# Transposed blocks in two alternating tiles, transposed one to two steps sooner: a two-layer encoder on one Trainium2 core

## The chip, the cores and the metric

The kernel runs on one core of a Trainium2 chip. A core has a matrix engine (TensorE, PE in the profile), a vector engine (VectorE, DVE), an engine for activations and casts (ScalarE, ACT), GpSimd (POOL) and SyncE (SP). Each works through its own queue in order, and they wait for each other by semaphores. Transfers between the core's memory and the device's run on 16 DMA engines; SP issues most of them and GpSimd those that add to what lies at the target. Beside ScalarE, VectorE and GpSimd prepare operands and TensorE multiplies into banks of its accumulator memory, which the others empty.

The metric is the device time in microseconds (us) of one execution; the median of several runs counts.

## What is computed

A sequence of 512 tokens with 1024 features passes two layers. The first has a stick-breaking attention, the second a gated linear recurrence; both end in the same multilayer perceptron (MLP), and a last norm follows. Cut to what matters here:

```python
for layer in range(DEPTH):
    h = rms_norm(x, norm_mix[layer])
    y = mixer(layer, h)
    x = x + y
    h = rms_norm(x, norm_mlp[layer])
    x = x + squared_relu_mlp(h, mlp_w1[layer], mlp_w2[layer])
return rms_norm(x, norm_final)

def squared_relu_mlp(h, w1, w2):
    u = jax.nn.relu(h @ w1)
    return (u * u) @ w2
```

The change lies in the second layer's MLP, at `x = x + ...`: the `x` that is added there.

## The kernel before

**Numbers.** Everything is float32. A product is made of three matmuls with operands split into a high half (a cast on ScalarE) and a low half (operand less high half, on VectorE), lines 242 to 246 and 1079 to 1086. So every 512 KB of weights cost a cast of 1.05 us on ScalarE and a subtraction of 1.2 us on VectorE.

**The MLP (class `Mlp`).** The 4096 hidden features are taken in four quarters of 1024. Quarter one's hidden features are computed ahead of the loop. Then `run` (line 1156) walks a list of 98 steps: 14 "down" steps of quarter one (steps 0 to 13), and for each further quarter 14 "up" steps (`h @ w1`, hidden features; two parts of seven products) and 14 "down" steps (`@ w2`). Quarter two has steps 14 to 41, quarter three 42 to 69, quarter four 70 to 97. The place of a step is counted here from its quarter's first: step 45 has place 3. The products follow a scheme of Strassen's kind: seven products P1 to P7 of quarter-size blocks stand for eight, with sums of operands before and sums of results after. In the up steps they come as P1, P5, P6, P3, P7, P2, P4, at places 0 to 6 for the first part and 7 to 13 for the second.

**One step.** For step i the loop (line 1344) calls `load(i)`, then `leave(i - 1)`, then issues TensorE's matmuls of step i. `load(i)` first runs what stands in the dictionary `aside` for step i, then issues due weight loads. `leave(i - 1)` empties the result of the step before (copies and relus on ScalarE, sums of results on VectorE, into tile `u`; later low halves go to `bl` and `sl`) and prepares the weight operand of step i + 3, with its cast (`wh`), its low half (`wl`), the sum of two weight blocks for the next product (`b<-b,b` on VectorE) or an addition to a weight block by DMA from GpSimd (line 1101). From the middle of quarter one, VectorE's and ScalarE's instructions of this loop are held in the order in which they are written (class `Ordered`, which gives line 786 to all of them in the profile). SP's and GpSimd's queues are ordered by the scheduler.

**The blocks of x.** The MLP's inputs and hidden features lie with features along partitions; the results `c` (`mlp.y(t, h)`) lie with tokens along partitions. So `x`, which has to be added to the result, must be transposed. It is parked in the device's memory (`away`, line 1667) while the MLP begins, and comes back in eight blocks of 128 tokens by 512 features, each in three stages, all hung into `aside` by the loop at line 1697:

- `fetch(n, a)`, four times: SP brings a quarter of block n back as pieces of 32 by 32, so placed that a transposition inside each 32 by 32 square completes the whole. Even blocks come to the end of `bh`, odd ones to the end of `bl`.
- `turned(n)`: VectorE transposes the 32 by 32 squares into a tile (`blocks`), 128 by 512 numbers. Before, this was one tile for all, of tag `osum` with one buffer.
- `joined(n)`, two steps later: GpSimd issues a DMA of 256 KB that adds the tile to the result (`c<-blocks` in the profile).

`BY_BLOCKS` holds for each block (first step of its fetches, fetches per step, step of its turn). As one tile serves all blocks, the turn of block n + 1 cannot start before the copy (`joined`) of block n has landed; and a fetch to `bh` or `bl` waits for the turn two blocks before. A turn stands in VectorE's order ahead of everything that `leave` of the step before issues.

Of the kernel before, what the change touches and what calls it, by code (L numbers as in the profile page):

```python
# [12 lines left out]
F32 = mybir.dt.float32  # L13
# [5 lines left out]
P = 128  # L19
S = 512  # L20
D = 1024
C = D // P
# [8 lines left out]

BLOCK = 32
BY_BLOCKS = (
    (12, 2, 16), (14, 1, 19), (17, 1, 23), (29, 1, 43), (33, 1, 46), (44, 1, 50), (57, 1, 71), (61, 1, 74),
)
START = [
# [31 lines left out]
def hybrid_encoder(  # L68
# [28 lines left out]
    work = ctx.enter_context(tc.tile_pool(name="work", bufs=2))  # L97
# [212 lines left out]
    HOMES = (*(("keep", 4),) * 4, *(("w3", 3),) * 3, ("osum", 1))  # L310

    def home_tile(tag, n, name):
        return home.tile([P, S], F32, tag=tag, name=name, bufs=n)
# [1349 lines left out]
    with ExitStack() as mctx:  # L1663
# [4 lines left out]
        blocks = {}  # L1668
# [18 lines left out]

        def turned(n):

            to = home_tile(*HOMES[C - 1], "blocks")  # L1690
            mlp.V.transpose(out=to, in_=blocks[n])
            blocks[n] = to

# [3 lines left out]
        for n, (at, by, done) in enumerate(BY_BLOCKS):  # L1697
            for a in range(P // BLOCK):
                mlp.aside.setdefault(at + a // by, []).append(partial(fetch, n, a))
            mlp.aside.setdefault(done, []).append(partial(turned, n))  # L1700
            mlp.aside.setdefault(done + 2, []).append(partial(joined, n))
# [171 lines left out]
```

## Time and profile before

| | us |
|---|---|
| median of 3 runs (1030.94 to 1031.68) | 1031.47 |
| the profiled execution | 1032.85 |
| its span, first to last instruction | 1031.0 |
| TensorE busy | 1019.2 |
| VectorE busy | 858.9 |
| ScalarE busy | 715.2 |
| the eight transpositions, each | 0.70 to 0.71 |
| the eight copies `c<-blocks`, issue to landing | 4.0 to 9.2, median 5.7 |

The copies, in order of blocks, took 8.6, 6.9, 4.0, 9.2, 5.5, 4.7, 5.9 and 4.6 us from issue to landing.

How to read the rows: a row of the timeline has the start and the length in us, the engine, the line of the kernel, the operation, what is written and read with the size, the count, and in brackets how long the engine idled before it and which instruction ended that wait. A row of the chain has start, length, engine, tile and line. "DMA to landing" gives the least, the median and the most us from issue to landing of the transfers that were asked for. In a row of windows there are, behind the stretch and its length, the busy time and count of TensorE's matmuls, its weight loads, VectorE, ScalarE and GpSimd, then the granted clock of TensorE, the DMA engines' busy share and GB/s. On VectorE and ScalarE the next instruction often starts a tenth before the one ahead ends.

### The profile page before, as it was taken

Reading aid. Unit: us, or ns where it says so; the run is one execution under the profiler, and the core shown is the slowest. Engines: PE = TensorE matmul, PEld = TensorE weight load, DVE = VectorE, ACT = ScalarE, POOL = GpSimd, SP = SyncE. Lnnn points to the kernel's source line nnn. Section 1 sums busy time; section 2 is a strip of 40 time slices with the busy share of each in tenths; the row PEclk is TensorE's granted clock in tenths of the full one; section 3 lists DMA queues with packets and bytes.
Section 4 is the critical chain, followed back from the end, with each engine's and each line's share of the span. In section 5 each row is a group of like instructions: output and inputs, shape, how many; then the busy total and the mean of one; then the engine's idle time right before and its main releaser. Section 6 shows DMA issues by size and latency. Waiting matters only on the chain.

```text
span 1031.0 us, 15905 instructions
## 1 busy us (share of the span) xinstructions
PE 1019.2 (99%) x5836; PEld 888.6 (86%) x5836; DVE 858.9 (83%) x1152; ACT 715.2 (69%) x1110; POOL 180.6 (18%) x243
## 2 busy tenths in 40 slices
PE   9999999999999999999999999999999999899997
PEld 7888888888878988988988888888888988888986
DVE  7888787847897798898899889984877898798898
ACT  6777676835877774874875689964876774674865
POOL 0354444420010010010012111300011111111112
PEclk9999999999999999999999999999999999999999
DMA  7845454537546677677682574364457977977753
GB/s 234 219 121 144 110 151 105 152 109 268 150 92 185 165 165 194 169 153 195 166 226 82 147 169 124 103 232 152 107 108 199 213 167 197 189 159 196 185 122 107
DMA packets 71902, 165.72 MB, mean 161 GB/s; under 512 B 23824, under 2 KB 25104, under 8 KB 71824
## 3 DMA queue, kind: packets, MB, share of 16 engines
q1 hardware_dynamic: 59424, 123.54, 37.7%
q0 software_dynamic: 11680, 40.38, 23.2%
q8 instruction: 46, 0.75, 0.3%
q10 hardware_dynamic: 720, 0.79, 0.2%
q14 instruction: 32, 0.26, 0.1%
HBM read 139.51 MB, written 6.29 MB: 141 GB/s over the span
## 4 chain that ended last, share of the span: by engine, by line
PE 87%; DVE 6%; ACT 3%; DMA 3%; issue 2%; SPq 0%; DVEq 0%; ACTq 0%
PE ps_t L1119 15%; PE ps_acc L1119 8%; PE ps_acc L1024 7%; PE ps_z L1024 6%; PE ps_acc L244 5%; PE ps_acc L246 5%; PE ps_acc L245 5%; PE ps_z L1119 4%; PE ps_o L1024 3%; PE ps_t L244 2%; PE ps_t L245 2%; PE ps_t L246 2%; PE ps_o L244 2%; PE ps_o L245 2%; PE ps_o L246 2%
## 5 line engine op out<-in xcount | busy, mean ns | idle before, releaser
L786 DVE TENSOR_TENSOR wl<-b,wh 128x1024 fp32r<-128x1024 f32 x168 | 203.9, 1219 | 48.7 <-ACT wh L786 47.7
L786 ACT CAST wh<-b 128x1024 fp32r<-128x1024 f32 x168 | 174.1, 1050 | 99.4 <-DVE b L786 57.3
L1101 POOL DMA_DIRECT2D b<-in_w_dn x40 | 35.1, 877 | 336.0 <-DVE b L786 143.7
L244 PE MATMUL ps_acc<-xg,wh 128*128 128x512 f32 x200 | 81.7, 408 | 0.0
L1024 PE MATMUL ps_z<-xg,wh 128*128 128x256 f32 x384 | 79.2, 278 | 1.8 <-ACT u L786 1.7
L246 PE MATMUL ps_acc<-xg,wh 128*128 128x512 f32 x200 | 78.4, 392 | 0.0
L245 PE MATMUL ps_acc<-xg,wl 128*128 128x512 f32 x200 | 78.4, 392 | 0.0
L239 DVE TENSOR_TENSOR wl<-raw,wh 128x512 fp32r<-128x512 f32 (+2 forms) x70 | 61.6, 905 | 16.2 <-ACT wh L237 16.1
L786 ACT ACTIVATE u<-u 128x512 f32<-128x512 f32 x100 | 63.2, 632 | 15.2 <-DVE u L786 13.5
L609 DVE TENSOR_TENSOR_SCAN scan<-keep,later 128x128 f32<-128x128 f32 (+1 forms) x64 | 58.7, 919 | 17.1 <-ACT keep L599 10.7
L237 ACT CAST wh<-raw 128x512 fp32r<-128x512 f32 (+2 forms) x70 | 50.7, 759 | 24.6 <-PE ps_acc L246 7.3
L1024 PE MATMUL ps_z<-xg,wl 128*128 128x256 f32 x240 | 66.4, 277 | 0.0
L1024 PEld LDWEIGHTS ps_z<-xg,wh 128*128 128x128 f32 x384 | 62.8, 188 | 2.4 <-ACT u L786 2.4
L1024 PE MATMUL ps_acc<-xg,wh 128*128 128x256 f32 x288 | 61.5, 277 | 1.1 <-ACT u L786 1.1
L613 POOL TENSOR_TENSOR w<-w,scan 128x128 f32<-128x128 f32 (+1 forms) x64 | 51.7, 809 | 53.8 <-DVE scan L609 50.8
L786 DVE TENSOR_TENSOR b<-b,b 128x1024 f32<-128x1024 f32 x48 | 58.7, 1223 | 1.3
L1101 POOL DMA_DIRECT2D b<-in_w_up x24 | 20.9, 871 | 215.6 <-DMA b<-in_w_up 86.3
L786 DVE TENSOR_TENSOR u<-u 128x512 f32<-128x512 f32 (+1 forms) x92 | 54.7, 594 | 2.4 <-ACT u L786 1.1
L1024 PE MATMUL ps_acc<-xg,wl 128*128 128x256 f32 x192 | 53.1, 276 | 0.0
L786 ACT CAST wh<-raw 128x1024 fp32r<-128x1024 f32 x46 | 47.9, 1044 | 7.3 <-PE ps_acc L1119 7.3
L1024 PE MATMUL ps_acc<-low,wh 128*128 128x256 f32 x192 | 53.0, 276 | 0.0
L1119 PE MATMUL ps_t<-wh,sl 128*128 128x512 f32 x126 | 49.3, 392 | 0.3 <-DVE sl L786 0.3
(372 smaller groups left out, 3276.2 us busy)
## 6 DMA issues: line engine op xcount, KB each, us to landing
b<-in_w_dn SPq DMA_DIRECT2D x48, 512.0 KB, 5.0
b<-in_w_dn POOLq DMA_DIRECT2D x40, 512.0 KB, 5.6
b<-in_w_up SPq DMA_DIRECT2D x36, 512.0 KB, 4.4
b<-in_w_up POOLq DMA_DIRECT2D x24, 512.0 KB, 5.5
raw<-in_w_m SPq DMA_DIRECT2D x16, 512.0 KB, 4.5
raw<-in_w_dn SPq DMA_DIRECT2D x16, 512.0 KB, 4.7
raw<-in_w_in SPq DMA_DIRECT2D x16, 512.0 KB, 4.4
raw<-in_w_qk SPq DMA_DIRECT2D x12, 512.0 KB, 3.8
```

Of the source, the lines that this page charges most:

```text
L237: A.copy(wh[:, k, :], raw[:, k, :])
L239: V.tensor_tensor(wl[:, k, :], raw[:, k, :], f(wh[:, k, :]), ALU.subtract)
L244: PE.matmul(ps, wh, ah, start=start, stop=False)
L245: PE.matmul(ps, wl, ah, start=False, stop=False)
L246: PE.matmul(ps, wh, al, start=False, stop=stop)
L609: V.tensor_tensor_scan(sc[:, S - n : S][:, ::-1], keep[:, :n][:, ::-1], later[:, S - n :][:, ::-1], 1.0, ALU.mult, ALU.max,)
L613: G.tensor_tensor(wt, wt, sc[:, S - n + 1 : S + 1], ALU.mult)
L786: ins = getattr(self.e, name)(*args, **kwargs)
L1024: PE.matmul(ps[:, i * HS : (i + 1) * HS], m, y, start=new and i == k == n == 0, stop=i == 1 and k == C // 2 - 1 and n == 2, skip_group_che ...
L1101: G.dma_start(out=unit[b].rearrange("p j n -> p (j n)"), in_=unit["src"](to), accum_op=ALU.add)
L1119: PE.matmul(ps, m, y[:, jj, cols], start=first and n == 0, stop=last and n == 2, skip_group_check=not new,)
```

## The change

Blocks with an odd number are transposed into a tile of another tag, `ssq`, with one buffer, which served the sum of squares before the loop. Even blocks keep the tile of before. Five of the eight turns come one or two steps sooner, and with each its copy, which stays two steps behind.

```diff
 BY_BLOCKS = (
-    (12, 2, 16), (14, 1, 19), (17, 1, 23), (29, 1, 43), (33, 1, 46), (44, 1, 50), (57, 1, 71), (61, 1, 74),
+    (12, 2, 16), (14, 1, 18), (17, 1, 21), (29, 1, 43), (33, 1, 45), (44, 1, 48), (57, 1, 71), (61, 1, 73),
 )
@@
         def turned(n):
 
-            to = home_tile(*HOMES[C - 1], "blocks")
+            if n % 2:
+                to = work.tile([P, S], F32, tag="ssq", name="blocks", bufs=1)
+            else:
+                to = home_tile(*HOMES[C - 1], "blocks")
             mlp.V.transpose(out=to, in_=blocks[n])
             blocks[n] = to
```

In places: block 0 stays at 2, block 1 goes from 5 to 4, block 2 from 9 to 7 (quarter two); block 3 stays at 1, block 4 goes from 4 to 3, block 5 from 8 to 6 (quarter three); block 6 stays at 1, block 7 goes from 4 to 3 (quarter four).

## The prediction

> **What bounds the kernel now.** I read the page first, for the bound of the whole, then the timeline of TensorE in layer two's multilayer perceptron, to measure its quarters one against the other.
>
> ```profile
> PE 1019.2 (99%) x5836; PEld 888.6 (86%) x5836; DVE 858.9 (83%) x1152; ACT 715.2 (69%) x1110; POOL 180.6 (18%) x243
> PE 87%; DVE 6%; ACT 3%; DMA 3%; issue 2%; SPq 0%; DVEq 0%; ACTq 0%
> ...
> 788.91 0.28 PE L1024 MATMUL ps_acc<-xg,wh 128*128 128x256 f32 x1
> ...
> 866.83 0.28 PE L1024 MATMUL ps_acc<-xg,wh 128*128 128x256 f32 x1
> ...
> 947.25 0.28 PE L1024 MATMUL ps_acc<-xg,wh 128*128 128x256 f32 x1
> ...
> 961.06 2.72 PE ps_z L1024 x24
> ```
>
> TensorE is the bound, and the chain leaves it for some 13% of the span. The three matmul rows are the first ones of steps 14, 42 and 70, so quarter two lasts 866.83 - 788.91 = 77.92 us and quarter three 80.42. A step is 24 matmuls in 2.72 us (last row), and 28 steps are 76.16. So quarter two loses 1.76 us and quarter three 4.26. That is the most that these two can give. Where quarter three loses them stands in the timelines of VectorE, TensorE and GpSimd:
>
> ```profile
> 872.05 0.89 POOL L1695 DMA_DIRECT2D c<-blocks  x1 [2.21 <-DVE blocks L786]
> ...
> DMA to landing us min/median/max: 9.2/9.2/9.2
> ...
> 876.81 1.23 DVE L786 TENSOR_TENSOR wl<-b,wh 128x1024 fp32r<-128x1024 f32 x1 [0.36 <-ACT wh L786]
> 881.29 0.71 DVE L786 STREAM_TRANSPOSE blocks<-bh 128x512 f32<-128x512 f32 x1 [3.25 <-DMA c<-blocks]
> 881.92 0.65 DVE L786 TENSOR_TENSOR u<-ps_acc,u 128x512 f32<-128x512 f32 x1
> ...
> 884.43 0.38 PE L1024 MATMUL ps_acc<-xg,wh 128*128 128x256 f32 x1 [1.06 <-ACT u L786]
> ...
> 893.89 0.39 PE L1024 MATMUL ps_z<-xg,wh 128*128 128x256 f32 x1 [0.99 <-ACT u L786]
> ...
> 900.33 0.39 PE L1024 MATMUL ps_z<-xg,wh 128*128 128x256 f32 x1 [0.71 <-ACT u L786]
> ```
>
> The turn of block 4 idles VectorE for 3.25 us: it writes the one tile that the copy of block 3 (issued at 872.05, landed 9.2 later, at 881.25) still reads. Behind it, in VectorE's fixed order, stands the subtraction of step 45, whose product TensorE had ended at 866.83 + 4 x 2.72 = 877.71. ScalarE follows with the relu, and TensorE then waits three times for a bank that ScalarE empties late. The three waits are 2.76 us; the first matmuls behind each, slower than the rest, and tenths elsewhere make up the 4.26.
>
> How much lateness VectorE may have is read by laying quarter four over it, where nothing waits for a copy:
>
> ```profile
> 957.23 1.23 DVE L786 TENSOR_TENSOR wl<-b,wh 128x1024 fp32r<-128x1024 f32 x1 [0.36 <-ACT wh L786]
> 958.48 0.71 DVE L786 STREAM_TRANSPOSE blocks<-bl 128x512 f32<-128x512 f32 x1
> 959.11 0.65 DVE L786 TENSOR_TENSOR u<-ps_acc,u 128x512 f32<-128x512 f32 x1
> ...
> 833.53 0.68 DVE L786 TENSOR_TENSOR sl<-u,sh 128x512 fp32r<-128x512 f32 x1
> ...
> 913.95 0.68 DVE L786 TENSOR_TENSOR sl<-u,sh 128x512 fp32r<-128x512 f32 x1
> ...
> 990.55 0.68 DVE L786 TENSOR_TENSOR sl<-u,sh 128x512 fp32r<-128x512 f32 x1
> 991.33 0.46 PE L1119 MATMUL ps_t<-wh,sl 128*128 128x512 f32 x1
> 991.63 0.40 PE L1119 MATMUL ps_t<-wh,sh 128*128 128x512 f32 x1
> ```
>
> Counted from each quarter's first matmul, the low half `sl` that the third down step needs starts at 44.62, 47.12 and 43.30 us. Quarter four's TensorE meets it almost without a gap (990.55 + 0.68 = 991.23, then 991.33 and 991.63). So VectorE and ScalarE, which hand work to each other from the first subtraction to this one, have no slack over TensorE there: what a turn adds to their chain, TensorE loses. Quarter three is 3.82 us behind quarter four, quarter two 1.32.
>
> **The change part by part.** Nothing is added in number: eight turns and eight copies stay, each turn 0.63 us from its start to the next instruction (881.29 to 881.92). Odd blocks get their own tile, and five turns move.
>
> *Block 4, place 4 to 3.* It now waits for the copy of block 2, over since long, and stands before the instruction at 876.81. VectorE idled there from 876.45, so the turn fills those 0.36 us, and the weight's low half starts at 876.45 + 0.63 = 877.08. From such a low half to the subtraction it is 1.15 us where nothing comes between (800.30 to 801.45, below), so that starts at 878.23, after the 877.71 of TensorE. Against 881.92 that is **3.69 us earlier**.
>
> *Block 5, place 8 to 6.*
>
> ```profile
> 888.49 0.68 DVE L786 TENSOR_TENSOR u<-u,ps_z 128x512 f32<-128x512 f32 x1
> 889.74 1.23 DVE L786 TENSOR_TENSOR wl<-b,wh 128x1024 fp32r<-128x1024 f32 x1 [0.58 <-ACT wh L786]
> ...
> 895.25 0.70 DVE L786 STREAM_TRANSPOSE blocks<-bl 128x512 f32<-128x512 f32 x1
> 895.88 2.83 DVE L786 TENSOR_TENSOR u<-u 128x512 f32<-128x512 f32 x4
> ```
>
> Before, it stood in a stretch without idle time and cost its whole 0.63. Now it stands ahead of 888.49, with 0.58 us of VectorE's idle time right behind. The low half at 889.74 does not move; ScalarE's relu, which needs the sum of 888.49, becomes some 0.2 us later. So it costs 0.2 (between 0 and 0.63). Together the `sl` of quarter three comes at 913.95 - 3.69 - 0.43 = 909.83, that is 43.00 after its first matmul, 0.30 before quarter four's. TensorE then no longer pays the 3.82 by which quarter three was behind quarter four. I take **3.7 us gained**, as some tenth may stay, between 3.1 (the turn is not absorbed) and 4.1 (all but 0.16 of the 4.26).
>
> *Block 7, place 4 to 3.* The same move without a wait: 957.23 - 0.36 + 0.63 + 1.15 puts the subtraction of 959.11 at 958.65, 0.46 earlier. But quarter four has only 991.63 and two like gaps of a tenth behind it to win: **0.2 gained**, between 0 and 0.5.
>
> *Block 1, place 5 to 4.*
>
> ```profile
> 800.30 1.23 DVE L786 TENSOR_TENSOR wl<-b,wh 128x1024 fp32r<-128x1024 f32 x1 [1.77 <-ACT wh L786]
> 801.45 0.68 DVE L786 TENSOR_TENSOR u<-ps_acc,u 128x512 f32<-128x512 f32 x1
> ...
> 803.30 1.23 DVE L786 TENSOR_TENSOR b<-b,b 128x1024 f32<-128x1024 f32 x1
> 804.44 0.70 DVE L786 STREAM_TRANSPOSE blocks<-bl 128x512 f32<-128x512 f32 x1
> ...
> 805.64 1.23 DVE L786 TENSOR_TENSOR wl<-b,wh 128x1024 fp32r<-128x1024 f32 x1
> ...
> 804.55 1.06 ACT L786 CAST wh<-b 128x1024 fp32r<-128x1024 f32 x1 [0.61 <-DVE b L786]
> ```
>
> Here the move looks bad. The turn was free: it ran at 804.44 while VectorE would have waited for ScalarE's cast (804.55 to 805.61) anyway. Now it stands ahead of 801.45, and the addition of 803.30, the cast and the low half of 805.64 all come 0.63 later. No idle time of VectorE follows that takes it up, since the chain runs hand to hand. **0.6 lost**, between 0 and 0.63.
>
> *Block 2, place 9 to 7.* It moves from behind the four sums to ahead of the low half before them. VectorE's total is the same; ScalarE's cast of the sums comes 0.63 later, and the bank it then empties too, so a small wait of TensorE grows there, but the later `sl` decides: 0, between 0 and 0.63 lost.
>
> *Queues.* The copies come one or two steps earlier on GpSimd's queue, and the fetches behind them on SP's. SP's fetch for blocks 3, 4, 6 and 7 waits for turns 1, 2, 4 and 5, so it too is issued up to 4 us earlier. On SP that can only free what stands behind it. The transfers join weights in a dense stretch; I take 0 and price it as a rival.
>
> One page of the Trainium skill disagrees with the row that all hangs on. DMA: Bandwidth & Descriptors, section Anatomy of one DMA, gives 2.0 us plus bytes / 436e3 for a DMA of GpSimd's queue. By an estimate from it, 256 KB land in 2.6 us, block 3's copy would have been over at 874.7, and the second tile would gain nothing. The trace has 9.2 and the 3.25 of waiting, and the measurement decides.
>
> The sum: -3.7 - 0.2 + 0.6 = **-3.3 us**. The profiled execution (1032.85, span 1031.0) would become 1029.55 with a span of 1027.7; it lies 1.38 over the median of 1031.47, from which I forecast 1031.47 - 3.3 = 1028.2.
>
> **The rivals.**
>
> *A new wait of block 5 (10%).* Its turn moves to 888.49 - 3.69 = 884.80.
>
> ```profile
> L1681 SPq DMA_DIRECT2D bl<-away x4: 326/484/691, 871.7 to 873.3; - x4
> ...
> DMA to landing us min/median/max: 6.3/8.3/8.9
> ...
> 885.37 0.87 POOL L1101 DMA_DIRECT2D b<-in_w_up  x1 [2.09 <-DVE b L786]
> ...
> DMA to landing us min/median/max: 5.6/5.6/5.6
> ...
> 895.37 1.05 ACT L786 CAST wh<-b 128x1024 fp32r<-128x1024 f32 x1
> ...
> 800.00:815.00 15.00, 15.00 (x134) 14.98 (x133) 12.56 (x13) 11.98 (x18) 2.64 (x3) 1.00 0.99 222
> ```
>
> Its four fetches are issued from 871.7 to 873.3 (first row) and land after 8.9 at most: by 882.2. The tile it now shares with block 3 is free at 881.25. The slack is 2.6 us. Were the landings 4 us longer, TensorE would lose 1.4 and the time be 1029.6. Against it: what competes is issued later than the fetches.
>
> *Quarter two pays nothing (12%).* If the 0.63 is hidden after all, as in its old place: 1031.47 - 3.9 = 1027.6.
>
> *Slower: the weight additions come late (8%).* In the dense stretches (DMA busy 0.99 from 800 to 815) earlier fetches and copies push back the additions that GpSimd issues to weights. In quarter three the one at 885.37, moved to 881.7, must land before its cast at 895.37 - 3.7 = 891.7: 10.0 us instead of the 5.6 shown, and about the 9.2 of block 3's copy. So it decides from landings over 10.0. To eat 3.3 us it must land after 13.3; at 16 the time is 1031.47 + 2.7 = 1034.2. Against it: here, among the copies and fetches of quarter three, it took 5.6. The same Trainium skill page, section Issuing engines are not separate DMA queues, says that all queues run on the same engines and interleave, which is the mechanism; the trace agrees so far that block 3's copy takes 9.2 us there, and shows no price beyond it.
>
> *The wait is not the tile's (7%).* Were the 3.25 due to something that stays, quarter two's loss and quarter four's gain alone were left: 1031.47 + 0.4 = 1031.9. Against it: 872.05 + 9.2 meets 881.29 to 0.04. By the fit of the Trainium skill quoted above, this is what would happen.
>
> **How the numbers follow.** The forecast has 63%; its own range runs from -4.1 - 0.3 = -4.4 (1027.1) to -3.1 + 1.2 = -1.9 (1029.6). The rivals have 10, 12, 8 and 7. The range to hold the time takes in free quarter two and most of block 5's wait: 1026.8 to 1030.2; outside lie the slower case, the unremoved wait and a few per cent of tails. A measurement tells some 0.2%, 2.1 us, from no change: faster is below 1029.4. That takes the forecast without its weakest tenth (57), free quarter two (12) and a third of block 5's case (4): 0.73. Slower takes 0.07, the rest 0.20.
>
> **What would show it.** Right: no idle time put to the copy before any turn; block 4's turn right before the low half that stood at 876.81; the three waits of TensorE in quarter three gone and its length near 76.7 us; quarter two near 78.5, longer than before; quarter four's gap at the third down step gone. Wrong: a turn of block 5 waiting for its fetch, a cast of ScalarE waiting for a weight addition, or a quarter three still near 80.

## The result, and the profile after

The changed kernel took 1029.5 us in the median of 14 runs (1028.48 to 1030.71), the kernel before 1031.13 in as many: a ratio of 0.9983 with a 95% interval of 0.9975 to 0.9991, or 0.9 to 2.6 us less. The forecast was 1028.2, 3.3 us less. The sign and the places were as forecast; the size was about half. The median lies inside the range that was to hold it (1026.8 to 1030.2), but a tenth over the 1029.4 below which the prediction had put a chance of 0.73. A later timing of the same kernel (`e7_after`, below) gave 1028.87 against 1031.51, a ratio of 0.9977 (0.9967 to 0.9987).

The profiled execution of the changed kernel took 1029.78 us with a span of 1027.9; for this one execution the prediction had 1029.55 and 1027.7. The first matmuls of steps 14, 42 and 70 in its timeline:

```profile
789.47 0.28 PE L1024 MATMUL ps_acc<-xg,wh 128*128 128x256 f32 x1
...
867.52 0.28 PE L1024 MATMUL ps_acc<-xg,wh 128*128 128x256 f32 x1
...
944.12 0.28 PE L1024 MATMUL ps_acc<-xg,wh 128*128 128x256 f32 x1
```

Quarter two takes 867.52 - 789.47 = 78.05 us, against 77.92 before, and quarter three 76.60, against 80.42 before and the 76.16 of 28 steps without a gap. From here to the end of the span it is 83.78, before it was 83.75. So quarter three gives 3.8 us, as forecast, and quarter two takes 0.1 back; it was forecast near 78.5. The rest of the difference between the spans, 0.56 us against the change, had arisen before step 14.

Now VectorE's timeline of quarter three, in the places that the prediction went through:

```profile
875.93 1.22 DVE L786 TENSOR_TENSOR wl<-raw,wh 128x1024 fp32r<-128x1024 f32 x1
877.06 0.70 DVE L786 STREAM_TRANSPOSE blocks<-bh 128x512 f32<-128x512 f32 x1
877.69 1.18 DVE L786 TENSOR_TENSOR wl<-b,wh 128x1024 fp32r<-128x1024 f32 x1
878.79 0.68 DVE L786 TENSOR_TENSOR u<-ps_acc,u 128x512 f32<-128x512 f32 x1
...
885.75 0.70 DVE L786 STREAM_TRANSPOSE blocks<-bl 128x512 f32<-128x512 f32 x1
886.38 0.65 DVE L786 TENSOR_TENSOR u<-u,ps_z 128x512 f32<-128x512 f32 x1
887.01 1.22 DVE L786 TENSOR_TENSOR wl<-b,wh 128x1024 fp32r<-128x1024 f32 x1
889.90 1.76 DVE L786 TENSOR_TENSOR bl<-u,bh 128x1536 fp32r<-128x1536 f32 x1 [1.67 <-ACT bh L786]
...
910.81 0.68 DVE L786 TENSOR_TENSOR sl<-u,sh 128x512 fp32r<-128x512 f32 x1
```

The reader is to see three things. No turn has a bracket: neither waits. Block 4's turn stands where VectorE had idled, and the subtraction follows 878.79 - 867.52 = 11.27 us after the quarter's first matmul, where it was 15.09 before (881.92 - 866.83). Block 5's turn takes the place of the idle time ahead of 887.01. The `sl` of the third down step comes at 43.29 after the first matmul; the forecast had 43.00. TensorE's rows agree: none of the three waits of quarter three is left, and from step 14 on there is a single one, the last row below.

Quarter two pays, also in the forecast place:

```profile
800.42 1.23 DVE L786 TENSOR_TENSOR wl<-b,wh 128x1024 fp32r<-128x1024 f32 x1 [1.33 <-ACT wh L786]
801.56 0.70 DVE L786 STREAM_TRANSPOSE blocks<-bl 128x512 f32<-128x512 f32 x1
802.19 0.65 DVE L786 TENSOR_TENSOR u<-ps_acc,u 128x512 f32<-128x512 f32 x1
802.77 1.20 DVE L786 TENSOR_TENSOR wl<-b,wh 128x1024 fp32r<-128x1024 f32 x1
804.01 1.23 DVE L786 TENSOR_TENSOR b<-b,b 128x1024 f32<-128x1024 f32 x1
805.15 0.68 DVE L786 TENSOR_TENSOR u<-u 128x512 f32<-128x512 f32 x1
806.35 1.23 DVE L786 TENSOR_TENSOR wl<-b,wh 128x1024 fp32r<-128x1024 f32 x1 [0.52 <-ACT wh L786]
...
820.61 0.39 PE L1024 MATMUL ps_z<-xg,wh 128*128 128x256 f32 x1 [0.71 <-ACT u L786]
```

Block 1's turn stands between the low half and the subtraction, and the 0.52 us of waiting for ScalarE's cast, which the turn filled before, is back ahead of 806.35. The last row, of TensorE, is the small wait that block 2's sooner turn was to make; `e6_block1_back` below, with block 2's turn sooner and block 1's not, has it too (0.51 us), and it costs no length there.

### The profile page after: what moved, and what is told of

Its sections match the earlier page's. It is cut to its first block, busy times and chain, and to the rows that moved or that the text cites. A ratio compares the mean times of both kernels' runs of the same rounds, so it can differ in the third digit from the quotient of the medians.

```text
span 1027.9 us, 15902 instructions
## 1 busy us (share of the span) xinstructions
PE 1017.9 (99%) x5836; PEld 888.2 (86%) x5836; DVE 859.1 (84%) x1152; ACT 715.4 (70%) x1110; POOL 180.5 (18%) x243
## 4 chain that ended last, share of the span: by engine, by line
PE 90%; DVE 4%; DMA 3%; ACT 2%; issue 1%; SPq 0%; ACTq 0%; DVEq 0%
PE ps_t L1119 16%; PE ps_acc L1024 8%; PE ps_acc L1119 8%; PE ps_z L1024 7%; PE ps_acc L244 5%; PE ps_acc L246 5%; PE ps_acc L245 5%; PE ps_o L1024 4%; PE ps_z L1119 4%; PE ps_t L245 2%; PE ps_t L244 2%; PE ps_t L246 2%; PE ps_o L244 2%; PE ps_o L245 2%; PE ps_o L246 2%; PE ps_t L631 2%
```

## The experiments

The forecast took the ledger of one profiled execution of the kernel before off the median of its runs, and got the half of it. Two theories. **A:** the wait of block 4's turn differs from execution to execution, and the profiled one had a long one. **B:** the wait is always as long, and the changed kernel gives something back outside quarter three. Beside it the parts of the change were taken apart.

### The kernel before, three more profiles; the changed one, one more

`b1_before` and `b2_before`, no edit:

> The kernel before once more, for a second profiled execution. Theory A: the copy of block 3 lands sooner than 9.2 us, the wait of block 4's turn is 0 to 2.5 us, and quarter three is 77.5 to 79.5 us. Theory B: the wait is again 3.0 to 3.5 us and quarter three 80.4.

> A third profiled execution of the kernel before: as for the second.

`b4_before`, no edit, run later:

> A fourth profiled execution of the kernel before. Theory A: block 3's copy lands after 7.2 to 8.2 us, block 4's turn waits 1.3 to 2.3 us and quarter three is 78.5 to 79.5 us; the 9.2 us of the first profile was the rare one.

`b3_after`, the changed kernel, no edit:

> The changed kernel once more. Both theories: no turn waits, quarter three 76.6 us again. Theory A: quarter two 77.5 to 78.5, by the landing of its weight addition. Theory B: steps 0 to 13 or quarter two again later than in before by 0.5 us or more.

Block 4's turn in VectorE's timeline and the landing of block 3's copy, of `b1_before`, then `b2_before`, then `b4_before`:

```profile
878.59 0.71 DVE L786 STREAM_TRANSPOSE blocks<-bh 128x512 f32<-128x512 f32 x1 [1.87 <-DMA c<-blocks]
...
DMA to landing us min/median/max: 7.8/7.8/7.8
```

```profile
878.92 0.71 DVE L786 STREAM_TRANSPOSE blocks<-bh 128x512 f32<-128x512 f32 x1 [1.51 <-DMA c<-blocks]
...
DMA to landing us min/median/max: 7.4/7.4/7.4
```

```profile
879.31 0.71 DVE L786 STREAM_TRANSPOSE blocks<-bh 128x512 f32<-128x512 f32 x1 [2.79 <-DMA c<-blocks]
...
DMA to landing us min/median/max: 8.7/8.7/8.7
```

Block 7's turn in `b1_before`:

```profile
956.36 0.71 DVE L786 STREAM_TRANSPOSE blocks<-bl 128x512 f32<-128x512 f32 x1 [0.58 <-DMA c<-blocks]
```

All times in this table are us, worked out from the timelines as above: the quarters from the first matmuls of steps 14, 42 and 70, "quarter four" from that of step 70 to the end of VectorE's last instruction, "out" from there to the end of the span, which holds the last stores.

| execution | block 3's copy lands after | block 4's turn waits | quarter two | quarter three | quarter four | out |
|---|---|---|---|---|---|---|
| before | 9.2 | 3.25 | 77.92 | 80.42 | 79.97 | 3.78 |
| b1_before | 7.8 | 1.87 | 77.63 | 79.05 | 80.53 | 3.80 |
| b2_before | 7.4 | 1.51 | 77.73 | 78.71 | 80.13 | 3.75 |
| b4_before | 8.7 | 2.79 | 77.47 | 79.97 | 80.58 | 3.83 |
| after | 7.8 | 0 | 78.05 | 76.60 | 79.76 | 4.02 |
| b3_after | 7.6 | 0 | 78.10 | 76.62 | 79.76 | 3.99 |
| e7_after | 7.2 | 0 | 78.19 | 76.61 | 79.77 | 4.02 |

Theory A holds. Quarter three of the kernel before less the wait is 77.17, 77.18, 77.20 and 77.18 us: the length follows the wait one for one, over a spread of 1.7 us, and the wait follows the landing. Theory B's 3.0 to 3.5 us in every execution did not come; the 9.2 us of the first profile was the longest of four. But 8.7 came too, so "rare", as expected of the fourth, is too much said. Quarter four had a wait that the first profile did not show, of block 7's turn for block 6's copy: 0.58 us in `b1_before`, 0.20 in `b2_before` and 0.64 in `b4_before`. That makes it differ in length from 79.97 to 80.58: less the wait it is 79.95, 79.93 and 79.94 us, and 79.97 where no wait shows. Even there it was close, as block 6's copy, issued at 952.46, landed 5.9 us later, at 958.36, and the turn started at 958.48.

Quarter two differs as well, from 77.47 to 77.92 before and from 78.05 to 78.19 after, though no turn waits in it. A cast of ScalarE does, for an addition to a weight that GpSimd issues 3.5 us after the first matmul of step 14 and that landed after 6.3 to 6.7 us in these seven executions. The cast in `before`, then in the changed kernel:

```profile
799.22 1.05 ACT L786 CAST wh<-b 128x1024 fp32r<-128x1024 f32 x1 [1.31 <-DMA b<-in_w_up]
```

```profile
799.34 1.05 ACT L786 CAST wh<-b 128x1024 fp32r<-128x1024 f32 x1 [0.87 <-DMA b<-in_w_up]
```

Counted from the start of the low half behind this cast (800.30 and 800.42) to the first matmul of step 42, quarter two takes 66.50 to 66.53 us in the four executions of before and 67.10 to 67.11 in the three of the changed kernel. With this landing taken out, the change costs quarter two 0.6 us in every execution, as forecast.

### The changed kernel once more, timed

> The changed kernel, timed once more against before on the same chip. From its first matmul of step 14 to the end, the four profiled executions of before take 242.1, 241.0, 240.3 and 241.9 us and the two of the changed kernel 238.4 and 238.5: a difference of 2.9 us. Theory A1 (what the quarters show is what the runs gain, and the 1.6 us between the first medians was low by the scatter of the first 60 us): the median is 2.2 to 3.2 us under before. Theory A2 (outside the profiled executions the wait is shorter still): 1.2 to 2.0 us under before.

Measured: 1028.87 us against 1031.51, 2.6 us less, inside A1's 2.2 to 3.2; its interval of 0.9967 to 0.9987 is 1.3 to 3.4 us and does not exclude A2 by itself. By the means of the table, the changed kernel gains 2.9 us in quarter three (79.54 to 76.61) and 0.5 in quarter four (80.30 to 79.76), and loses 0.4 in quarter two (77.69 to 78.11) and 0.2 at the end (3.79 to 4.01): 2.8 in all. The starts of step 14 scatter: 787.85 to 788.91 us in the four executions of before and 788.01 to 789.47 in the three of the changed kernel, in which 0.5 of the 2.8 are lost in the mean. The interval of the first timing, 0.9 to 2.6 us, does not reach the 2.8; that of the second does.

### Two tiles, the old steps

```diff
-    (12, 2, 16), (14, 1, 18), (17, 1, 21), (29, 1, 43), (33, 1, 45), (44, 1, 48), (57, 1, 71), (61, 1, 73),
+    (12, 2, 16), (14, 1, 19), (17, 1, 23), (29, 1, 43), (33, 1, 46), (44, 1, 50), (57, 1, 71), (61, 1, 74),
```

(against the changed kernel)

> Two alternating tiles, turns at the steps of before. Theory A (the wait on the copy was longer in the profiled execution of before than it mostly is; the ledger by quarters holds): no turn waits for a copy; quarter three is 77.3 us (quarter four's chain plus 0.63 for block 5 in its old place), quarter two 77.9, quarter four as before; some 2 us of the 3.3 us wait stay gone in any execution, and the median is 1.0 to 1.5 us under before. Theory B (the wait is as long in every execution, and the changed kernel gives back 1.5 us outside quarter three): this version gives nothing back and is 3.0 us or more under before.

Measured: 1029.55 us, ratio to before 0.9985 (0.9976 to 0.9993), quarters of 77.56 and 77.09 us. As theory A has it: the second tile alone brings 1.5 us, where the whole change brought 1.6 in the first timing. Quarter three is 0.5 us longer than in the changed kernel, quarter two 0.5 shorter than there. From step 14 to the end of VectorE's last instruction this version takes 234.50 us, the changed kernel 234.41, 234.48 and 234.57: what the sooner turns gain in quarters three and four they lose in quarter two, and on balance they bring nothing.

### One tile, the new steps

```diff
-    (12, 2, 16), (14, 1, 19), (17, 1, 23), (29, 1, 43), (33, 1, 46), (44, 1, 50), (57, 1, 71), (61, 1, 74),
+    (12, 2, 16), (14, 1, 18), (17, 1, 21), (29, 1, 43), (33, 1, 45), (44, 1, 48), (57, 1, 71), (61, 1, 73),
```

(against the kernel before)

> One tile, turns at the new steps. Both theories: three turns now run into copies. By the landings of the profile of before, block 1's turn, ready at 801.5, waits until 803.0 (1.5 us), block 4's, ready at 876.45, until 881.25 (4.8 us), block 7's 1.5 us. Quarter two is 1.5 to 2 us longer than before, quarter three 0.7 longer, quarter four loses 1 us; the median is 2 to 4 us over before. If the sooner steps alone made the gain, it would be at or under before.

Measured: 1035.9 us, 4.9 over before, more than the 2 to 4 expected; ratio 1.0045 (1.0033 to 1.0058). From step 14 to the end of the span the profiled execution is 3.5 us over the mean of before (244.77 against 241.32); the rest of the 4.9 is not explained. The turns of blocks 1, 4 and 7 in VectorE's timeline:

```profile
803.20 0.71 DVE L786 STREAM_TRANSPOSE blocks<-bl 128x512 f32<-128x512 f32 x1 [1.98 <-DMA c<-blocks]
...
881.90 0.71 DVE L786 STREAM_TRANSPOSE blocks<-bh 128x512 f32<-128x512 f32 x1 [3.06 <-issue]
...
960.27 0.71 DVE L786 STREAM_TRANSPOSE blocks<-bl 128x512 f32<-128x512 f32 x1 [2.03 <-issue]
```

All three wait. "issue" is the profile's word for a wait whose end it cannot assign; block 3's copy, issued at 874.43, landed after 7.4 us, at 881.83, just ahead of 881.90, and block 6's, issued at 953.83, after 6.4, at 960.23. Quarter two is 80.09 us and quarter four 81.52. Quarter three, 79.40, is 0.7 us longer than the 78.71 of `b2_before`, in which the copy landed after 7.4 us too: the 0.7 expected, once executions with like landings are compared. The sooner steps are only to be had with the second tile.

### Blocks 1 and 2 back, and block 1 alone back

```diff
-    (12, 2, 16), (14, 1, 18), (17, 1, 21), (29, 1, 43), (33, 1, 45), (44, 1, 48), (57, 1, 71), (61, 1, 73),
+    (12, 2, 16), (14, 1, 19), (17, 1, 23), (29, 1, 43), (33, 1, 45), (44, 1, 48), (57, 1, 71), (61, 1, 73),
```

> The changed kernel with blocks 1 and 2 put back to their old steps 19 and 23 (two tiles; quarters three and four as changed). Forecast's step: block 1's move costs 0.6 us. If so, VectorE's chain of quarter two, from the start of its first low half of a raw operand's successor to the third down step, is 0.6 us shorter than in the changed kernel, the quarter is 77.4 us and the median 0.6 us under the changed one. Rival: quarter two's length hangs on when its weight addition lands, and the move costs nothing: quarter and median as changed.

Measured: quarter two 77.57 us (78.05 to 78.19 in the changed kernel), the `sl` of its third down step at 44.27 us from the first matmul instead of 44.76 to 44.89; quarters three and four as changed (76.58 and 79.78). Median 1027.99, ratio 0.9974 (0.9964 to 0.9984). The quarter shows 0.5 of the 0.6; counted from the low half behind the late cast, it is the whole 0.6 (66.52 us, as before, against 67.10 to 67.11). The medians of the two timings differ by 1.5 us (0.9 with the later timing of the changed kernel), more than the quarters show for this edit.

`e6_block1_back` puts only block 1 back:

```diff
-    (12, 2, 16), (14, 1, 18), (17, 1, 21),
+    (12, 2, 16), (14, 1, 19), (17, 1, 21),
...
```

> The changed kernel with only block 1's turn put back from step 18 to 19. Forecast's step: block 1's move is the whole loss of quarter two and block 2's costs nothing: quarter two 77.5 to 77.6 us as with both put back, its third down step's low half at 44.2 to 44.3 us from its first matmul. Rival: block 2's sooner turn costs too: quarter two 77.8 or more.

Measured, in one execution: quarter two 77.60 us, the low half at 44.29; from the low half behind the late cast again 66.52 us. Block 1's move is the whole loss, block 2's costs nothing.

### One tile, two turns one step later

```diff
-    (12, 2, 16), (14, 1, 19), (17, 1, 23), (29, 1, 43), (33, 1, 46), (44, 1, 50), (57, 1, 71), (61, 1, 74),
+    (12, 2, 16), (14, 1, 19), (17, 1, 23), (29, 1, 43), (33, 1, 47), (44, 1, 50), (57, 1, 71), (61, 1, 75),
```

(against the kernel before)

> One tile as before; only block 4's turn goes from step 46 to 47 and block 7's from 74 to 75, that is from place 4 to 5, where VectorE waits for a cast of ScalarE. Theory (the gain is the wait, and a turn at place 5 comes some 2.3 us later than the copy's landing of 7 to 8 us needs): no turn waits or one by a few tenths, quarter three is 77.0 to 77.4 us (block 5 still costs its 0.63), quarter two 77.6 to 77.8, and the median is 1.2 to 2.2 us under before, as much as with two tiles. Rival (the second tile itself is needed): a wait of 1 us or more stays and the median is at most 0.5 us under before.

Measured: 1029.18 us against 1031.4, ratio 0.9977 (0.9968 to 0.9986); quarters of 77.36 and 76.98 us. The place in VectorE's timeline:

```profile
878.70 1.23 DVE L786 TENSOR_TENSOR wl<-b,wh 128x1024 fp32r<-128x1024 f32 x1 [0.39 <-DMA bl<-away]
879.96 1.22 DVE L786 TENSOR_TENSOR b<-b,b 128x1024 f32<-128x1024 f32 x1
881.10 0.70 DVE L786 STREAM_TRANSPOSE blocks<-bh 128x512 f32<-128x512 f32 x1
881.73 0.65 DVE L786 TENSOR_TENSOR u<-u 128x512 f32<-128x512 f32 x1
882.30 1.23 DVE L786 TENSOR_TENSOR wl<-b,wh 128x1024 fp32r<-128x1024 f32 x1
```

Block 3's copy (871.70, landed after 7.5) is over at 879.2, and the turn at 881.10 does not wait. The second tile is not what is needed: to put the turn behind three instructions more does as much. From step 14 to the end of VectorE's work this version takes 234.10 us, against 234.41 to 234.57 with the whole change and 236.57 to 238.31 before.

### Two tiles, turns where VectorE waits for ScalarE anyway

```diff
-    (12, 2, 16), (14, 1, 18), (17, 1, 21), (29, 1, 43), (33, 1, 45), (44, 1, 48), (57, 1, 71), (61, 1, 73),
+    (12, 2, 16), (14, 1, 19), (17, 1, 20), (29, 1, 43), (33, 1, 47), (44, 1, 48), (57, 1, 71), (61, 1, 75),
```

(against the changed kernel)

> Two tiles; the second turn of each quarter at place 5, where VectorE has to wait for a cast of ScalarE anyway, the third at place 6: steps 19, 20, 47, 48, 75. Theory: a turn at place 5 costs nothing, at place 3 it cost 0.27, at place 4 0.63; the third at place 6 costs 0.2. Quarter two is 76.9 to 77.3 us (its weight addition's landing stays in it), quarters three and four as changed, and the median 0.6 to 1.2 us under the changed kernel. Rival: the earlier fetch of block 3 and copy of block 2 fall into the dense stretch of transfers and delay the weight additions: quarter two 78 us or more, median at or over the changed one.

> The version with turns at places 5 and 6, beside the changed kernel on the same chip. From step 14 to the end its first trace has 237.7 us against 238.4 and 238.5: the median is 0.5 to 1.1 us under the changed kernel's, 3 to 4 us under before if A1 holds, 2 to 3 if A2 does.

Measured: 1028.04 us the first time, ratio 0.997 (0.9958 to 0.9982), and 1028.39 the second, 0.9968 (0.9958 to 0.9979), where the changed kernel on the same chip had 1028.87. Quarter two is 77.30 and 77.10 us, quarters three and four are 76.59 and 76.64, 79.77 and 79.77. Quarter two of `e8_hidden`:

```profile
803.81 0.70 DVE L786 STREAM_TRANSPOSE blocks<-bl 128x512 f32<-128x512 f32 x1
804.44 0.65 DVE L786 TENSOR_TENSOR u<-u 128x512 f32<-128x512 f32 x1
805.02 1.23 DVE L786 TENSOR_TENSOR wl<-b,wh 128x1024 fp32r<-128x1024 f32 x1
806.28 1.23 DVE L786 TENSOR_TENSOR b<-b,b 128x1024 f32<-128x1024 f32 x1
807.43 0.70 DVE L786 STREAM_TRANSPOSE blocks<-bh 128x512 f32<-128x512 f32 x1
808.06 0.65 DVE L786 TENSOR_TENSOR u<-u,ps_z 128x512 f32<-128x512 f32 x1
808.68 1.23 DVE L786 TENSOR_TENSOR wl<-b,wh 128x1024 fp32r<-128x1024 f32 x1
```

Two turns are in, and VectorE waits for ScalarE at neither low half: the turns lie in the idle time. In the quarters this is 0.9 us better than the change. Quarter two has it all: from the low half behind the late cast it takes 66.11 and 66.12 us, 0.6 less for block 1 and 0.4 less for block 2, whose turn at place 6 costs less than at place 7 or 9. In the medians of the same chip it is 0.48, just under the 0.5 to 1.1 expected and too little for the intervals to separate; against before it is 3.1, at the lower edge of A1's 3 to 4. It is the lowest of the versions in both timings that it had beside others but for `e3_q2old`, which was level with it. The rival, that the earlier transfers delay weight additions, shows in part and costs nothing: quarter two's third addition landed after 7.1 us in both (5.2 to 6.4 before), and no cast waits for it.

## Why the prediction was right, and where its size was off

- *The wait of block 4's turn is the tile's, and goes.* Right. No turn waits in the changed kernel; the single tile brings the waits back as soon as the turns are sooner (`e2_steps`), and they vanish without a second tile when the turns are later (`e5_one_tile`). That rules out the rival by which the wait would stay.
- *Quarter three gains 3.7 us.* The mechanism was right, the place too, and the length after (76.7 forecast, 76.60 to 76.62 measured) as well. **The mis-sized term is this one:** 3.7 was the loss of one execution, and the sum took it off the median of the runs. In four executions the loss was 2.1 to 3.8, in the mean 2.9. Most of that is the wait, 2.4 in the mean, which the second tile takes away alone; the sooner turns of blocks 4 and 5 add 0.5 (77.09 in `e1_tiles` to 76.60). The prediction had the warning in hand, since it noted that the profiled execution lay 1.38 us over the median, and did not ask whether the term it was about to remove was where the 1.38 lay. The copy's 9.2 us was a single landing, next to a median of 5.7 for all eight.
- *Block 5 costs 0.2 at its new place.* Right as far as it shows: the low half at 887.01 came at 19.49 us from the first matmul, where quarter four, without a block 5, has it at 19.49 (963.61 - 944.12), and the next one of VectorE 0.2 later (22.38 against 966.31 - 944.12 = 22.19). So its move gains about 0.4: quarter three is 76.98 us with its turn at the old place (`e5_one_tile`) and 76.59 and 76.64 at the new one (`e4_hidden`, `e8_hidden`), block 4's turn standing at place 5 in all three. It waited for no fetch, so that rival did not come.
- *Block 7 gains 0.2.* The move itself is worth 0.1 to 0.2, as forecast: in the changed kernel quarter four is 79.76 us, before, less the wait, 79.93 to 79.97, and with the second tile and the old steps (`e1_tiles`) 79.85. The term was too small all the same: in three of four executions of before this turn waited too, and quarter four gained 0.2 to 0.8, in the mean 0.5. That nothing waits for a copy there, as the prediction says, held in the first profile alone, and there by a tenth. Again one execution stood for all.
- *Block 1 loses 0.6, block 2 nothing.* Right: 0.6 counted from the low half behind the late cast, and nothing for block 2. In whole quarters it is 0.4 in the mean and 0.5 by putting block 1 back, since that low half came at other times. In the two first profiles the loss shows as 0.1 only, because the low half ahead of the turn waited 1.33 us after and 1.77 before.
- *The weight additions come late: slower.* The additions did come later, but not late enough. The one that the prediction names landed after 8.4, 8.7 and 9.0 us in the three executions of the changed kernel, against 5.6 to 8.2 in the four of before. In the first of the three it was issued at 882.64, landed at 891.04, and its cast started at 892.83, so a landing of 10.2 was the limit, near the 10.0 of the prediction. No cast of quarter three waits for an addition, but the margin was 1.2 to 1.8 us, and that the forecast escaped this rival was in part luck.
- *The range.* The lower end of the forecast's own range, -4.1 - 0.3, does not follow from its terms: with -0.5 for block 7 and 0 for block 1 it would be -4.6. Nothing measured lies there.
- *The ledger's remainder.* With the measured terms the sum is -2.9 - 0.5 + 0.4 + 0.2 = -2.8 us, and the two timings had 1.6 and 2.6. So the mis-sized terms explain why 3.3 was too much, but not why the first timing shows only 1.6. The 0.2 at the end stays open. Step 14 starts at 787.85 to 790.78 us over all executions that were profiled. By ScalarE's rows these differences arise in the first 360 us, in layer one: at `CAST bh<-u`, 358.19 us in `before`, each of the thirteen other executions is already off by what it is off at step 14, to within 0.1 us (the changed kernel by 0.52, `b4_before` by -1.04). The change acts only after step 14, so I take the starts for scatter; what scatters there was not tried.

## What to carry to other kernels

Before the cost of a wait on a transfer is taken off a median, look at it in more than one execution: a landing can differ by 1.8 us between executions of one kernel. Where two engines hand work to each other and both are near the bound, an instruction costs least in the place where its engine waits for the other's result anyway: here block 1's turn, 0.63 us long, cost 0.6 more one step sooner, and block 2's 0.4 more one or three steps later. Sooner is not better by itself; all that this change gained net came from the wait. And before a buffer is doubled, see whether the waiting instruction can stand behind the landing.

## What was not expected of the hardware

The same copy of 256 KB, issued 5.2 us after the first matmul of step 42 each time, landed after 7.4, 7.8, 8.7 and 9.2 us in four executions of one kernel, while the turn that waited for it took 0.71 us in all four. And from VectorE's end to the end of the span it took 3.75 to 3.83 us in the four executions of before, 3.99 to 4.02 in the three of the changed kernel, but 4.80, 4.67 and 4.73 in `e1_tiles`, `e5_one_tile` and `e6_block1_back`, though nothing near the end was edited. In these three the last store, of 256 KB, landed 3.7 us after ScalarE issued it, in all others after 2.7 to 2.8. What sets this was not tried.
